# Reordering the products of the whole Strassen pairs in a hybrid decoder step

## Chip, cores and metric

The kernel runs as one program on one core of a Trainium2 chip. The metric is device time in microseconds (us), the median of several runs; lower is better.

## What is computed

Two layers of a decoder trunk run for 512 prompt positions and 8 sample positions, 520 columns in all, with a model width of 2048. In each layer a normalised x is multiplied by `w_in` (2048 by 8192); half of the result goes through a short gated convolution, half through a four-head retention with a carried state; the two halves, joined, are multiplied by `w_out` (2048 by 2048) and added to x; then `x = x + sigmoid(x @ w_pg) * (p @ w_ple)`.

```python
z = h @ w_in
b_c, c_c, x_c, g_c, q, k, v, g_r = split_projection(z)
y_conv = b_c * conv_y * jax.nn.silu(g_c)
y_ret = (o * gn_g.astype(jnp.float32)).astype(x.dtype) * jax.nn.silu(g_r)
x = x + jnp.concatenate([y_conv, y_ret], axis=-1) @ w_out
x = x + jax.nn.sigmoid(x @ w_pg) * (p_i @ w_ple)
```

Everything is float32. The three large products take nearly all of the time.

## The kernel before

**Products.** A float32 operand is held as a high part and a rest, both in the type float32r, and each product of tiles is three matmuls (`mm3`, lines 247 to 249): high by high, high by rest, rest by high. Every such matmul has 128 by 128 weights and 260 moving columns (one half of the 520). Weights arrive from HBM as raw float32 tiles in `raw_ring` (32 tiles, so four loads of eight) and are split by `split_w`: ScalarE copies the high part (line 229), VectorE subtracts it (line 230); the parts wait in `split_ring` (60 tiles).

**Pairs.** Output tiles are made two at a time by `pair`. Each pair has a number of rows s that goes through one level of Strassen-Winograd (the function `strassen`): seven block products in place of eight. The rest of the 16 rows, or all 16 when s is 0 (`plain`), is multiplied in the ordinary way. A pair with s of 16, all its rows, is called whole here. The tables `CONVS`, `OUT_ROWS` and `GATES` make 47 of the pairs whole: 13 in the convolution part of each layer, 5 in the `w_out` part of each layer, 6 and 5 in the `w_pg` part. They stand in six unbroken chains.

**The seven products of a whole pair,** each of 24 matmuls (8 tiles, 3 matmuls a tile), go into three PSUM banks called a, b and d, out of five that the class `Banks` deals in the order in which they were given back:

| product | weights | bank | what follows in the text of the kernel |
|---|---|---|---|
| P1 | w11 | a | ScalarE copies a into d |
| P2 | w21 + w22 - ... | b | ScalarE copies b to the right half of z1 |
| P3 | combination | a, on top of P1 | ScalarE copies a to the right half of z0 |
| P4 | w12 | d, on top of the copy | ScalarE copies d to the left half of z0; one step of other work (`aside`) |
| P5 | w11 - w21 | a, on top | VectorE adds a to the right half of z1 |
| P6 | w12 - combination | b, on top | VectorE adds b to the right half of z0 |
| P7 | w22 | a, on top | ScalarE copies a to the left half of z1 |

Copies and additions out of PSUM are lines of the helpers `copy` and `plus`; both are recorded under line 307. The combinations of raw weights are made in place by VectorE (`add`, line 319). After P7 the three banks go back together, in the order d, b, a. A raw slot goes back when the last product that reads it has been split: w12 after P4, w11 after P5, w21 after P6, w22 after P7.

**What sets the order.** The kernel's text isn't the order of execution. The program is built with `schedule_with_timeline_sim=True`: a planner walks a simulated timeline and gives each engine its own order, by priority. A line that stands earlier in the text has the higher priority; splits of weights and weight sums are lifted by `WPRIO`, and copies and additions out of PSUM go to the front (`high_priority`). Each engine then executes its list in that order. So a product can start ahead of one that stands before it in the text when that one isn't ready in the simulation. Loads of weights are issued by SyncE (line 312 for Strassen pairs, line 222 for ordinary rows).

**Around the pairs.** `middle` and `later` are lists of small jobs (building operands of the next large product, loading and updating the sample group's state, retention steps, the small `w_ple` product) that `strassen` calls at fixed places of its text.

Of the kernel before, what the change touches and what calls it, by code (L numbers as in the profile page):

```python
# [15 lines left out]
KT = D // P  # L16
# [63 lines left out]
class Slots:  # L80
# [8 lines left out]
    def get(self, dtype=F32):  # L89
        i = self.free.pop(0)  # L90
        self.count += 1
        t = self.pool.tile([P, T], dtype, tag=f"s{i}", name=f"slot{i}_{self.count}")
        self.used[id(t)] = (t, i)
        return t
# [97 lines left out]
def trunk_kernel(  # L192
# [17 lines left out]
    get, getr, put = slots.get, slots.getr, slots.put  # L210
    raw_ring = Ring(const, RAW, F32, "raw", 8)
    split_ring = Ring(const, SPLIT, F32R, "split")
    banks = Banks(pg, 5)
# [11 lines left out]
    def split_w(raw, slot=False):  # L225
        n = raw.shape[1]
        hi, lo = (getr()[:, :n] if slot and not split_ring.fits(n // P) else split_ring.get(n // P) for _ in range(2))
        with tc.high_priority(offset=WPRIO):
            S.activation(hi, raw, AF.Copy)  # L229
            V.tensor_tensor(lo, raw, F(hi), SUB)  # L230
        return hi, lo

    def chunks(a, b, most=CH):

        n = (b - a + most - 1) // most
        e = [a + (b - a) * i // n for i in range(n + 1)] if n else [a]
        return list(zip(e, e[1:]))

    def parts(src, a, b, slot=False):
        raw = load(src[:, P * a : P * b])  # L240
        w = split_w(raw, slot)
        raw_ring.put(raw)
        return w
# [7 lines left out]
    LEFT, RIGHT = slice(0, TH), slice(TH, T)  # L251

    def product(out, w, c, xs, start, stop, more=False):

        for i, (xh, xl) in enumerate(xs):
            m = slice(P * (c + i), P * (c + i) + P)
            mm3(out, w[0][:, m], w[1][:, m], xh, xl, start and i == 0, stop and i == len(xs) - 1, more)

    def at(ops, ks, n):
        return [ops[k].view(n) for k in ks]  # L260

    def acc(n):
        return [banks.get() for _ in range(n)]

    def aside():

        if later:
            later.pop(0)()
# [18 lines left out]
        aside()  # L287
        return Val(banks.put, ps=ps[:2]), Val(banks.put, ps=ps[2:])

    def strassen(x, src0, src1, s, step=None):  # L290

        q = s // 2
        ops = x.ops
        x.supply(min(s + CH, KT))
        assert len(x.sums) >= q
        k1, k2 = at(ops, range(0, s, 2), LEFT), range(1, s, 2)
        t1, t2, t3, t4 = ([t[i] for t in x.sums[:q]] for i in range(4))
        step = step or (lambda n: None)  # L300
        a, b, d = acc(3)
        c = banks.get() if s < KT else None
        z0, z1 = get(), get()

        def early(fn, *args):
            with tc.high_priority():
                fn(*args)  # L307

        def raws(src, first):
            w = raw_ring.get(q)  # L310
            for i, j in chunks(0, q, CHL):
                DMA.dma_start(w[:, P * i : P * j], src[:, P * (first + i) : P * (first + j)])
            return w

        def add(out, x, y, op):
            for i, j in chunks(0, q, CHA):
                n = slice(P * i, P * j)
                with tc.high_priority(offset=WPRIO):
                    V.tensor_tensor(out[:, n], x[:, n], y[:, n], op)  # L319

        def times(out, raw, xs, start, more):
            for i, j in chunks(0, q, CHS):
                w = split_w(raw[:, P * i : P * j])
                product(out, w, 0, xs[i:j], start and i == 0, j == q, more)
                split_ring.put(*w)

        def copy(out, ps):
            early(S.activation, out, ps, AF.Copy)

        def plus(out, x, y):  # L330
            early(V.tensor_tensor, out, x, y, ADD)

        w11 = raws(src0, 0)
        times(a, w11, k1, True, False)
        step(1)
        copy(d, a)
        w21, w22 = raws(src1, 0), raws(src1, q)  # L340
        add(w11, w11, w21, SUB)
        add(w21, w21, w22, ADD)
        times(b, w21, t1, True, False)
        step(2)
        copy(z1[:, RIGHT] if c is None else c, b)
        add(w21, w22, w11, SUB)
        times(a, w21, t2, False, True)
        step(3)
        copy(z0[:, RIGHT], a)
        w12 = raws(src0, q)  # L350
        add(w21, w12, w21, SUB)
        times(d, w12, at(ops, k2, LEFT), False, True)
        raw_ring.put(w12)
        step(4)
        if c is None:
            copy(z0[:, LEFT], d)
        aside()
        times(a, w11, t3, False, True)
        raw_ring.put(w11)
        step(5)  # L360
        if c is None:
            plus(z1[:, RIGHT], a, z1[:, RIGHT])
        else:
            copy(z1[:, LEFT], a)
        while middle:
            middle.pop(0)()
        times(b, w21, at(ops, k2, RIGHT), False, True)
        raw_ring.put(w21)
        step(6)
        if c is None:  # L370
            plus(z0[:, RIGHT], b, z0[:, RIGHT])
        times(a, w22, t4, False, True)
        raw_ring.put(w22)
        step(7)
        for i, j in chunks(s, KT):
            last = j == KT
            x.supply(min(j + CH, KT))
            p1, p0 = parts(src1, i, j), parts(src0, i, j)
            product(c, p1, 0, at(ops, range(i, j), RIGHT), False, last, True)
            product(a, p1, 0, at(ops, range(i, j), LEFT), False, last, True)  # L380
            split_ring.put(*p1)
            product(d, p0, 0, at(ops, range(i, j), LEFT), False, last, True)
            product(b, p0, 0, at(ops, range(i, j), RIGHT), False, last, True)
            split_ring.put(*p0)
        if c is not None:
            plus(z1[:, RIGHT], c, z1[:, LEFT])
            copy(z0[:, LEFT], d)
            plus(z0[:, RIGHT], b, z0[:, RIGHT])
            banks.put(c)
        copy(z1[:, LEFT], a)  # L390
        banks.put(d, b, a)
        step(8)
        aside()
        return Val(put, slot=z0), Val(put, slot=z1)

    def pair(x, src, m, n, nxt=None):


        s = x.rows[n]
        last = n == len(x.rows) - 1 and nxt is not None  # L400
        if s:
            z = strassen(x, src[m], src[m + 1], s, (lambda i: x.free(i, nxt)) if last else None)
        else:
            z = plain(x, src[m], src[m + 1], (lambda a, b: x.free_tiles(a, b, nxt)) if last else None)
        x.release(n + 1)
        if nxt is not None and not last and not x.todo:
            nxt.fill(1, PRE)
        return z
# [14 lines left out]
    class Operands:  # L423


        def __init__(self, rows, load, reserve=0, whole=False, gain=None):
            self.rows, self.load, self.reserve, self.whole, self.gain = rows, load, reserve, whole, gain
            self.sent = []
            self.ops = [None] * KT
            self.sums = []  # L430
            self.ready = 0
            first = max(rows[0], min(FIRST, max(rows))) // 2
            self.todo = [(True, True)] * first + [(True, False)] * (KT // 2 - first)
            self.todo = [(i, *t) for i, t in enumerate(self.todo)]
            self.todo += [(i, False, True) for i in range(first, max(rows) // 2)]
# [239 lines left out]
    for a, b in ((0, 1), (1, 4), (4, 8), (8, 12), (12, 16)):  # L675
        raws = []
        if b == 1:
# [3 lines left out]
            x = get()  # L681
# [3 lines left out]
            w = split_w(raw)  # L685
            ws = [[t[:, P * m : P * m + P] for t in w] for m in range(4)]
        else:
            for i in range(4):
                raws.append(load(wi[0, i, :, P * a : P * b]))
                if i < b - a:  # L690
                    x = get()
# [24 lines left out]
    for l in range(DEPTH):  # L716
# [27 lines left out]
        def times(out, z, table):  # L744
            for n, v in z:
                V.tensor_tensor(out[:, n], v, table[:, n], MUL)  # L746
# [54 lines left out]
        def head(m):  # L801
            middle.append(lambda: X.fill(MORE_HEAD, 0))
            if m // 2 % 2:
                middle.append(sample)
            zs = pair(X, wi[l], m, m // 2 - skipped)
            X.fill(MORE_HEAD, 0)
            X.need(m // 2 - skipped + 1)
            sample()
            return zs
# [365 lines left out]
        for m in range(0, KT - tail, 2):  # L1175
# [19 lines left out]
            for i, z in enumerate(zs):  # L1195
                x = xs[i]
# [18 lines left out]
        if tail:  # L1215
            for t in Gt.sums:
                put(*t[4])
            ops = Gt.ops
# [27 lines left out]
            for j, n in enumerate(blocks):  # L1246
                c = slice(PC * j, PC * j + PC)
# [34 lines left out]
            for i in range(tail):  # L1282
                ps = banks.get(TF)
                for c, w in enumerate(ws):
                    for k in range(2):
                        o, m = ops[2 * c + k], slice(PC * k + P * i, PC * k + P * i + P)
                        mm3(ps, w[0][:, m], w[1][:, m], o.x[:, n0], o.y[:, n0], c + k == 0, c + k == 8)
                x = x2[m0 + i][:, n0]
# [38 lines left out]
            for j, n in enumerate(blocks):  # L1327
# [18 lines left out]
                c, q = slice(PC * j, PC * j + PC), slice(j, j + 1)  # L1346
                x = xts[:, c]
# [131 lines left out]
```

## Time and profile before

| | |
|---|---|
| three runs | 2167.43, 2169.55 and 2171.86 us, median 2169.55 |
| the profiled execution | span 2167.3 us, from its first to its last instruction; it has no other time of its own |
| TensorE matmul busy | 2147.8 us, 99% of the span, 17861 instructions |
| TensorE weight load busy | 2142.1 us |
| VectorE busy | 1896.1 us, 87% |
| ScalarE busy | 1264.5 us, 58% |
| GpSimd busy | 430.6 us, 20% |
| bytes moved by DMA | 387.31 MB, mean 179 GB/s |

The busy time of an engine is the union of its instructions' spans; matmul ends are modelled and overlap, so idle time under some 0.15 us between two matmuls doesn't show as idle. In rows of waits, an arrow names what ended the idle time.

### The profile page before, as it was taken

How to read it: one execution, taken by the hardware profiler on the slowest of the kernel's cores; microseconds unless marked ns; L12 is line 12 of the kernel's file. 1: busy time of each engine (PE TensorE's matmuls, PEld its weight loads, DVE VectorE, ACT ScalarE, POOL GpSimd, SP SyncE). 2: the span in 40 equal slices, each digit the busy share in tenths (PEclk: the TensorE clock that was granted, in tenths of full speed). 3: DMA queues.
4: the chain of work that ended last, by engine and by line, in shares of the span. 5: the costliest groups of instructions: out<-in, count | busy, mean ns of one | idle time of the engine just before them, and what ended most of it. 6: DMA issues, size and time to landing. Idle time of an engine off the chain costs nothing. (4 is left out here: it accounts for less than half of the span.)

```text
span 2167.3 us, 48178 instructions
## 1 busy us (share of the span) xinstructions
PE 2147.8 (99%) x17861; PEld 2142.1 (99%) x17861; DVE 1896.1 (87%) x3849; ACT 1264.5 (58%) x2647; POOL 430.6 (20%) x746
## 2 busy tenths in 40 slices
PE   9999999999999999999999999999999999999998
PEld 9999999999999999999999999999999999999998
DVE  8889988998999987987997988989999998879884
ACT  8656655565555655655765655565645555456565
POOL 2313222211001211200212222231111022011011
PEclk9999999999999999999999999999999999999999
DMA  8555565545543745645645566664464355566455
GB/s 288 171 175 197 181 217 184 178 157 175 158 129 118 238 156 187 215 154 160 215 144 175 172 213 191 189 209 170 151 182 149 120 158 202 176 207 200 128 164 198
DMA packets 182861, 387.31 MB, mean 179 GB/s; under 512 B 25888, under 2 KB 56352, under 8 KB 182624
## 3 DMA queue, kind: packets, MB, share of 16 engines
q1 hardware_dynamic: 128704, 212.98, 31.6%
q0 software_dynamic: 53056, 169.84, 23.8%
q8 instruction: 140, 2.29, 0.4%
q10 hardware_dynamic: 864, 1.39, 0.2%
q14 instruction: 97, 0.79, 0.1%
HBM read 318.96 MB, written 65.15 MB: 177 GB/s over the span
## 5 line engine op out<-in xcount | busy, mean ns | idle before, releaser
L247 PE MATMUL ps_g<-slot,split 128*128 128x260 f32 x5465 | 1531.6, 284 | 7.2 <-ACT slot L307 2.9
L248 PE MATMUL ps_g<-slot,split 128*128 128x260 f32 x5465 | 1534.3, 282 | 0.3 <-DVE slot L555 0.3
L249 PE MATMUL ps_g<-slot,split 128*128 128x260 f32 x5461 | 1519.9, 283 | 0.5 <-DVE split L230 0.5
L229 ACT ACTIVATE split<-raw 128x512 fp32r<-128x512 f32 (+2 forms) x1347 | 777.3, 596 | 583.1 <-DVE raw L319 213.2
L247 PEld LDWEIGHTS ps_g<-slot,split 128*128 128x128 f32 x5465 | 1024.0, 188 | 10.1 <-ACT slot L307 3.7
L248 PEld LDWEIGHTS ps_g<-slot,split 128*128 128x128 f32 x5465 | 1028.5, 188 | 0.5 <-DVE slot L555 0.5
L249 PEld LDWEIGHTS ps_g<-slot,split 128*128 128x128 f32 x5461 | 1019.8, 188 | 1.0 <-DVE split L230 1.0
L230 DVE TENSOR_TENSOR split<-raw,split 128x512 fp32r<-128x512 f32 (+2 forms) x1346 | 849.2, 652 | 172.5 <-PE ps_g L248 85.4
L319 DVE TENSOR_TENSOR raw<-raw 128x512 f32<-128x512 f32 (+1 forms) x660 | 428.9, 660 | 32.5 <-DMA raw<-wi 23.7
L307 ACT ACTIVATE slot<-ps_g 128x260 f32<-128x260 f32 x336 | 127.4, 381 | 140.6 <-PE ps_g L249 122.7
L551 ACT ACTIVATE slot<-slot 128x520 fp32r<-128x520 f32 (+1 forms) x212 | 109.2, 562 | 46.6 <-DVE slot L414 11.1
L552 DVE TENSOR_TENSOR slot<-slot,slot 128x520 fp32r<-128x520 f32 (+1 forms) x212 | 124.4, 620 | 4.1 <-ACT slot L551 3.9
L781 POOL DMA_DIRECT2D o_rets<-slot x64 | 35.3, 552 | 351.6 <-DVE slot L780 131.7
L307 DVE TENSOR_TENSOR slot<-ps_g,slot 128x260 f32<-128x260 f32 x168 | 70.9, 424 | 6.0 <-PE ps_g L249 3.7
L869 POOL DMA_DIRECT2D slot<-hs x64 | 46.2, 724 | 118.7 <-DVE split L230 42.7
L814 POOL DMA_DIRECT2D hs<-slot x64 | 35.6, 556 | 139.3 <-DVE slot L755 61.3
L780 DVE SCALAR_TENSOR_TENSOR slot<-slot,vs,slot 128x256 f32<-128x256 f32 x128 | 56.1, 481 | 4.5 <-ACT slot L776 4.3
L746 DVE TENSOR_TENSOR slot<-slot,slot 128x520 f32<-128x520 f32 x80 | 55.8, 698 | 4.7 <-DMA o_rets<-slot 3.7
L770 POOL DMA_DIRECT2D slot<-sret x64 | 35.5, 554 | 114.6 <-ACT split L229 37.3
L1058 POOL DMA_DIRECT2D slot<-x1s x76 | 40.8, 538 | 87.6 <-PE ps_g L249 27.2
L1209 POOL DMA_DIRECT2D x2s<-slot x30 | 16.4, 545 | 201.6 <-DVE slot L1204 200.6
L771 POOL DMA_DIRECT2D slot<-kq x64 | 34.9, 547 | 106.0 <-DVE slot L876 22.2
(217 smaller groups left out, 1733.8 us busy)
## 6 DMA issues: line engine op xcount, KB each, us to landing
raw<-wi SPq DMA_DIRECT2D x377, 256.0 KB, 3.9
raw<-wo SPq DMA_DIRECT2D x128, 256.0 KB, 5.4
raw<-wg SPq DMA_DIRECT2D x122, 256.0 KB, 4.1
raw<-wi SPq DMA_DIRECT2D x136, 192.0 KB, 4.0
slot<-x1s POOLq DMA_DIRECT2D x76, 260.0 KB, 5.1
slot<-sret POOLq DMA_DIRECT2D x64, 256.0 KB, 4.0
hs<-slot POOLq DMA_DIRECT2D x64, 256.0 KB, 4.0
slot<-hs POOLq DMA_DIRECT2D x64, 256.0 KB, 5.2
```

Source lines behind the costliest of these rows:

```text
L229: S.activation(hi, raw, AF.Copy)
L230: V.tensor_tensor(lo, raw, F(hi), SUB)
L247: PE.matmul(out, wh, xh, start=start, stop=False, skip_group_check=more)
L248: PE.matmul(out, wh, xl, start=False, stop=False, skip_group_check=more)
L249: PE.matmul(out, wl, xh, start=False, stop=stop, skip_group_check=more)
L307: fn(*args)
L319: V.tensor_tensor(out[:, n], x[:, n], y[:, n], op)
L551: keep(S.activation(hi, src[:, n], AF.Copy))
L552: V.tensor_tensor(lo, src[:, n], F(hi), SUB)
L746: V.tensor_tensor(out[:, n], v, table[:, n], MUL)
L780: keep(V.scalar_tensor_tensor(st[:, c], k, vs[:, h, e, b : b + 1], st[:, c], MUL, ADD))
L869: SIDE.dma_start(t[:, :512].rearrange("p (m n) -> p m n", m=2), src)
```

## The change

In a whole pair the sixth product P6 is put ahead of the fifth P5 in the text. The first product of the next pair (with its copy from a to d) is made by a function `begin`, and is called inside the present pair between P5 and P7 when the next pair is whole too (`ahead`), at least two banks are free, and the operands are there; the next pair then takes the two banks and the weights from `x.begun`. Bank d goes back right after its copy behind P4, b right after its addition behind P6, and a after P7. For pairs that aren't whole the order of the text stays, and so do all counts of instructions, bytes and sums. Of the 47 whole pairs, 41 are followed by a whole one.

```diff
-    def strassen(x, src0, src1, s, step=None):
+    def strassen(x, src0, src1, s, step=None, ahead=None):
...
+        whole = s == KT
...
-        a, b, d = acc(3)
-        c = banks.get() if s < KT else None
-        z0, z1 = get(), get()
-
...
-        w11 = raws(src0, 0)
-        times(a, w11, k1, True, False)
+        def begin(src):
+            a, d = acc(2)
+            w = raws(src, 0)
+            times(a, w, k1, True, False)
+            copy(d, a)
+            return a, d, w
+
+        a, d, w11 = x.begun or begin(src0)
+        x.begun = None
+        b = banks.get()
+        c = None if whole else banks.get()
+        z0, z1 = get(), get()
         step(1)
-        copy(d, a)
         w21, w22 = raws(src1, 0), raws(src1, q)
...
         if c is None:
             copy(z0[:, LEFT], d)
+            banks.put(d)
         aside()
+        if whole:
+            times(b, w21, at(ops, k2, RIGHT), False, True)
+            raw_ring.put(w21)
+            step(6)
+            plus(z0[:, RIGHT], b, z0[:, RIGHT])
+            banks.put(b)
         times(a, w11, t3, False, True)
         raw_ring.put(w11)
         step(5)
-        if c is None:
+        if whole:
             plus(z1[:, RIGHT], a, z1[:, RIGHT])
         else:
             copy(z1[:, LEFT], a)
         while middle:
             middle.pop(0)()
-        times(b, w21, at(ops, k2, RIGHT), False, True)
-        raw_ring.put(w21)
-        step(6)
-        if c is None:
-            plus(z0[:, RIGHT], b, z0[:, RIGHT])
+        if not whole:
+            times(b, w21, at(ops, k2, RIGHT), False, True)
+            raw_ring.put(w21)
+            step(6)
+        elif ahead is not None and len(banks.free) > 1 and all(ops[0:KT:2]):
+            x.begun = begin(ahead)
         times(a, w22, t4, False, True)
         raw_ring.put(w22)
         step(7)
...
             banks.put(c)
+            banks.put(d, b)
         copy(z1[:, LEFT], a)
-        banks.put(d, b, a)
+        banks.put(a)
...
-            z = strassen(x, src[m], src[m + 1], s, (lambda i: x.free(i, nxt)) if last else None)
+            z = strassen(x, src[m], src[m + 1], s, (lambda i: x.free(i, nxt)) if last else None,
+                         src[m + 2] if s == KT and x.rows[n + 1 : n + 2] == [KT] else None)
```

## Rows read from the trace of the kernel before

**Rows 1.** The page: busy time by engine; busy tenths and granted clock in 40 slices.

```profile
PE 2147.8 (99%) x17861; PEld 2142.1 (99%) x17861; DVE 1896.1 (87%) x3849; ACT 1264.5 (58%) x2647; POOL 430.6 (20%) x746
...
PEclk9999999999999999999999999999999999999999
```

**Rows 2.** Windows: six stretches with the 47 whole pairs; busy us (instructions), clock, DMA.

```profile
444.00:696.00 252.00, 251.06 (x2099) 250.88 (x2098) 230.61 (x458) 139.56 (x281) 32.93 (x47) 1.00 0.48 147
...
919.00:1057.00 138.00, 138.00 (x1154) 138.00 (x1154) 112.56 (x207) 78.80 (x151) 14.44 (x27) 1.00 0.51 159
1513.00:1766.00 253.00, 252.57 (x2105) 251.74 (x2104) 232.88 (x463) 139.06 (x282) 32.80 (x47) 1.00 0.48 146
...
sum 960.00, PE 958.46 PEld 957.25 DVE 832.99 ACT 526.33 POOL 119.31; mean PE 159.74 PEld 159.54 DVE 138.83 ACT 87.72 POOL 19.88
```

**Rows 3.** Waits of TensorE, whole span: us in total, times, longest.

```profile
PE ps_g L247 <- ACT slot L307: 2.9, 4, 1.3
PE ps_g L247 <- ACT ps_g L307: 1.6, 2, 1.2
...
PE ps_vt L913 <- DMA slot<-hs: 0.9, 1, 0.9
...
PE ps_g L247 <- DVE slot L307: 0.2, 1, 0.2
```

**Rows 4.** Waits of TensorE in the stretch from 1513 to 1766 us.

```profile
PE ps_g L247 <- ACT split L229: 0.2, 1, 0.2
```

**Rows 5.** Timeline of TensorE in a pair of `w_out`: start us, duration us.

```profile
868.40 0.28 PE L249 MATMUL ps_g<-slot,split 128*128 128x260 f32 x1
868.52 0.28 PE L247 MATMUL ps_g<-slot,split 128*128 128x260 f32 x1
```

**Rows 6.** Timeline of ScalarE, last whole pair of the first `w_out`: copies out of PSUM.

```profile
858.76 0.39 ACT L307 ACTIVATE slot<-ps_g 128x260 f32<-128x260 f32 x1 [0.80 <-PE ps_g L249]
...
861.64 0.39 ACT L307 ACTIVATE slot<-ps_g 128x260 f32<-128x260 f32 x1 [0.80 <-PE ps_g L249]
```

**Rows 7.** Timeline of VectorE, the same pair: the addition behind P5.

```profile
865.08 0.42 DVE L307 TENSOR_TENSOR slot<-ps_g,slot 128x260 f32<-128x260 f32 x1
```

**Rows 8.** Timeline of ScalarE, a whole pair of the first convolution and its neighbours' joins.

```profile
561.16 0.37 ACT L307 ACTIVATE slot<-ps_g 128x260 f32<-128x260 f32 x1
...
561.95 0.38 ACT L307 ACTIVATE ps_g<-ps_g 128x260 f32<-128x260 f32 x1
...
580.92 0.39 ACT L307 ACTIVATE slot<-ps_g 128x260 f32<-128x260 f32 x1 [0.58 <-PE ps_g L249]
...
581.73 0.38 ACT L307 ACTIVATE ps_g<-ps_g 128x260 f32<-128x260 f32 x1
```

**Rows 9.** The loads of line 312 from issue to landing: stretches 444 to 696, 770 to 870.

```profile
DMA to landing us min/median/max: 2.6/3.5/6.8
...
DMA to landing us min/median/max: 3.0/5.6/7.2
```

**Rows 10.** Waits of VectorE and ScalarE for TensorE: 820 to 900, then 560 to 660.

```profile
DVE split L230 <- PE ps_g L248: 8.4, 12, 0.8
...
ACT split L229 <- PE ps_g L249: 14.2, 12, 2.2
```

**Rows 11.** Waits of TensorE from 700 to 731 and from 1785 to 1797 us.

```profile
PE ps_g L247 <- ACT split L229: 1.3, 1, 1.3
PE ps_g L247 <- ACT ps_g L307: 1.2, 1, 1.2
PE ps_g L247 <- ACT slot L307: 0.8, 1, 0.8
...
PE ps_g L247 <- ACT slot L307: 1.9, 2, 1.3
```

**Rows 12.** Timeline of ScalarE ahead of the wait that ends at 706.46 us.

```profile
702.89 2.31 ACT L551 ACTIVATE slot<-slot 128x260 fp32r<-128x260 f32 x5
...
706.03 0.37 ACT L307 ACTIVATE ps_g<-ps_g 128x260 f32<-128x260 f32 x1
```

More of the change, by code (lines that the diff above doesn't have):

```diff
@@ L430, in __init__ @@
             self.sums = []
+            self.begun = None
             self.ready = 0
```

## The prediction

> **What bounds the kernel now.** I read the page first. TensorE is busy for 99% of the span with matmuls and as long with weight loads, VectorE for 87%, and the granted clock stands at the top of its scale in all 40 slices [rows 1]. So the question for any reordering is how much of TensorE's time is waiting, and where.
>
> The second view cuts the span into stretches. The change touches whole pairs alone, and the 47 of them lie in six stretches that I cut at their chains' ends: 960.00 us together, in which matmuls are busy for 958.46 us [rows 2]. The reader is to see the difference, 1.54 us: that is all the visible idle time of TensorE in every place that the change edits. In the stretches of `w_out` and in the first of `w_pg` there is none at all.
>
> The third view, the waits, names what is in those 1.54 us. The longest, 0.9 us, is a retention step that waits for a load of old keys and values (ps_vt); it has nothing to do with the pairs. What is left is 0.2 us for a split of weights [rows 4] and 0.2 us for VectorE's addition out of PSUM [rows 3]. The larger waits on copies out of PSUM in the list of the whole span, 2.9 and 1.6 us [rows 3], fall mainly elsewhere: 5.2 us of waits stand where the convolution's last pair ends and the first, ordinary pair of `w_out` begins, once in each layer [rows 11].
>
> A busy engine can still be slow inside, so the fourth view is the pitch from matmul to matmul: 868.40 to 868.52, 0.12 us [rows 5]. Two copies that stand behind two consecutive products of 24 matmuls start 858.76 and 861.64 us, 2.88 us apart, again 0.120 us a matmul [rows 6]: the join between two products in two banks costs nothing over the pitch. Seven products are 168 matmuls, 20.2 us a pair, and no order of products makes that less.
>
> **The change, part by part.**
>
> *Counts.* Matmuls, splits, weight sums, copies and bytes stay as they are: 0.
>
> *P6 ahead of P5, next P1 ahead of P7.* The planner already does much of this. In a convolution pair, the copy behind the old pair's P7 (561.16) and the copy of the new pair's a into d, which follows its P1 (561.95), start 0.79 us apart; at the other end of the pair they do so again, 580.92 and 581.73 [rows 8]. Were P1 executed after P7, they would stand at least 2.88 us apart. So the two products are already interleaved, and the new text mostly writes down an order that is being executed. What can be won is the wait of P7 for the addition behind P5: 0.2 us in the whole span [rows 3], taken as won: -0.2 us.
>
> *Banks given back early.* A new product waits for its bank only where the copies in the lists of waits stand; inside the six stretches no wait on line 307's copies by ScalarE is listed and the additions are the 0.2 us already counted. Worth 0. The Trainium skill (Perfetto Trace Analysis, section Matmuls) advises rotating independent groups through different banks so that evacuation overlaps the next group. By that rule more rotation should help; the trace says that three banks of five already hide every copy, so by the trace the sum gets nothing from it.
>
> *The ends of the chains.* This is where the change can cost. Six whole pairs have no whole successor, so there the text goes P6, P5, P7 with no P1 between, and P7 accumulates in bank a, which VectorE must first have read behind P5. Before, P6 covered that with 2.88 us. In the last whole pair of `w_out` P4's copy starts at 861.64 and P5 is the next product, so its result is ready for a reader at about 861.64 + 2.88 = 864.52; the addition runs from 865.08 for 0.42 us, to 865.50 [rows 6, 7]. Uncovered, that is 865.50 - 864.52 = 0.98 us of idle TensorE at each end, with P7 and everything behind it in TensorE's list held up; the longest wait of any kind on line 307 is 1.3 us [rows 3]. Six ends give between 0 (the planner fills the gap with the next pair's P1, an ordinary product, as it fills gaps today) and 6 x 1.3 = 7.8 us. I take 0.2 us each, the one wait on this addition that the trace shows, since the filler that the planner uses now is still there: +1.2 us.
>
> *The fourth load of a pair.* Four loads of eight tiles fill the raw ring, so w12 of the next pair goes into the slot of this pair's w22, which is free once P7's weights are split. In the old text three products (P1, P2, P3 of the next pair, 8.6 us) lie between that and P4; in the new one two (5.8 us), for P1 has gone ahead. A load of line 312 lands after a median of 3.5 us in the convolution and 5.6 in `w_out`, at most 6.8 and 7.2 [rows 9]. So most loads still fit, and some come up to 7.2 - 5.8 = 1.4 us late for the sum and the splits behind them. TensorE needn't see that: in `w_out` VectorE's splits wait for TensorE to give split slots back (8.4 us in 80), and in the convolution ScalarE's do (14.2 us in 100) [rows 10], so the splits run ahead of TensorE by as much as their ring holds. From 0 to 41 x 1.4 = 57 us; I take 0, for the ahead-running splits.
>
> *The queues.* The new P1 gets priority over P7 and over the arithmetic behind the pair. The loads of w11 move ahead with it on SyncE's queue, past none of the loads of the same pair. GpSimd's loads keep their place. VectorE has 960 - 833 = 127 us free in the stretches, ScalarE 434 [rows 2], and they get no more work: 0.
>
> Sum: 2167.3 - 0.2 + 1.2 = 2168.3 us for the span. The median of the runs was 2169.55, 2.25 us over the profiled span of 2167.3, so the time is 2170.5 us. Within 0.2%, 4.3 us, is about what a measurement of this kernel can't tell from no change; the three runs themselves spread over 4.4 us.
>
> **The rivals.**
>
> *Slower: uncovered additions at the ends of the chains.* The place is between P5 and P7 of six pairs, the price 0.98 to 1.3 us each. For it: TensorE takes matmuls in its list's order, and the planner's simulated delay need not be the chip's 0.98 us. The Trainium skill (PSUM - Partial Sum Buffer, section Engine vs sequencer instructions) says that matmuls start in program order, and the rows of waits agree: an idle TensorE ends with the one thing it waited for. Against it: the next pair's product is independent. With nothing filled, 6 x 1.3 = 7.8 us and 2177.4 us; it decides above 4.3 / 6 = 0.72 us an end.
>
> *Slower: w12 comes late.* Half a microsecond at each of the 24 convolution pairs with a whole successor would give 12 us, 2181.6 us; 0.18 us each already decides. Against it stand the medians of landing and the waits for split slots.
>
> *Slower: a new order brings a copy behind other work elsewhere.* The wait that ends at 706.46 shows the mechanism: ScalarE spent 2.31 us on five operand splits from 702.89, and the copy into bank d began only at 706.03 [rows 12]. Four such waits of 1.2 us more, 2174.4 us.
>
> *Faster: the 5.2 us behind the convolutions go.* The planner re-plans the whole program, and a change of priorities earlier may put those copies ahead of the operand splits. All of it gone would be 2169.55 - 5.2 = 2164.4 us. Against it: none of the lines edited stands there, since the pairs at that place are not whole.
>
> *Nothing happens.* If the planner arrives at nearly its old lists, 2169.5 us; this is on the same side as the forecast.
>
> **How the numbers follow.** No change within 0.2%: 0.62. Uncovered ends: 0.13. Late w12: 0.08. Copies behind other work: 0.05. Waits behind the convolutions gone: 0.12. So faster 0.12, same 0.62, slower 0.26. The range goes from 2163.5, just below the faster case, to 2178, over the first slower case; it leaves out late loads and the outer part of the others, some 0.15. The likeliest case's own range is 2166 to 2174.
>
> **What would show it.** Right: the six stretches keep TensorE idle for under 4 us in all, pairs follow each other every 20.2 us, the next pair's copy of a into d starts some 2.9 us ahead of the copy behind P7, and the granted clock stays at the top. Each step could be seen wrong: waits on the addition of line 307 at six places (ends of chains), waits of line 319 and line 229 on raw loads that pass on to TensorE (late w12), or a drop of the waits between the convolution and `w_out`. The prediction would be wrong if TensorE's time hid slack that no row here shows as idle, or if the re-planned lists differ far from the places edited.

## The result and the profile after

The changed kernel takes 2188.41 us (2185.0 to 2190.08, 4 runs) against 2169.03 us before, a ratio of 1.0088 with a 95% interval of 1.0073 to 1.0102: 19.4 us slower, outside the predicted range and on the side that had 0.26.

The page of the changed kernel (line 304 stands for the old 307, 316 for 319, 309 for 312). First its busy times, then the group of the weight sums (busy us, mean ns, idle us before them and what ended it):

```profile
PE 2155.3 (99%) x17861; PEld 2145.3 (98%) x17861; DVE 1895.9 (87%) x3849; ACT 1267.5 (58%) x2647; POOL 440.3 (20%) x746
...
L316 DVE TENSOR_TENSOR raw<-raw 128x512 f32<-128x512 f32 (+1 forms) x660 | 425.5, 655 | 76.5 <-DMA raw<-wg 42.7
```

The instruction counts are those of [rows 1], and VectorE works no longer than before. New is that VectorE stood idle for 42.7 us ahead of weight sums because weights of `w_pg` (wg) hadn't landed.

Windows of the changed kernel, columns as in [rows 2]: the first `w_pg` chain, then the first `w_out` chain.

```profile
924.00:1072.00 148.00, 144.31 (x1185) 142.29 (x1184) 115.87 (x219) 78.50 (x155) 15.79 (x30) 1.00 0.50 152
...
774.00:878.00 104.00, 104.00 (x869) 104.00 (x868) 79.41 (x135) 52.37 (x101) 13.45 (x25) 1.00 0.56 177
```

The same edit leaves no idle time in the `w_out` chain (104.00 of 104.00 us busy) and costs in `w_pg` (148.00 - 144.31 = 3.69 us idle, where [rows 2] has none). Waits of TensorE in the changed kernel, longest first:

```profile
PE ps_g L247 <- DVE slot L304: 5.0, 10, 1.8
PE ps_g L247 <- ACT slot L568: 4.5, 3, 2.6
PE ps_g L249 <- DVE split L230: 4.0, 8, 0.7
PE ps_g L247 <- ACT ps_g L304: 2.5, 2, 2.3
```

The wait of P7 for VectorE's addition went from 0.2 us [rows 3] to 5.0 us in ten places, and third matmuls of a tile (line 249, which read the rest of a weight) wait for VectorE's splits.

Visible idle time misses short delays, so I also summed, over all matmuls, how much later than 121 ns each started after the one before it, by the section of the program that it belongs to. This is worked out from the matmul starts in the trace (us; the names of the experiments are below):

```text
section            before  changed  own_ring  wp_first  others_old  old_own  late_start
layer 1 heads       10.93    10.78     11.29     10.63       10.35    10.82       10.93
layer 1 convolution  6.01     7.28      5.92      5.54        5.41     4.97        3.31
layer 1 w_out        3.58     6.65      7.00      6.72        5.33     4.96        7.20
layer 1 w_pg         1.41     7.85      1.48      1.44        5.37     1.15        1.15
layer 2 heads        5.80     9.23     10.04      8.20        8.18     5.98        7.27
layer 2 convolution  6.86     4.87      4.96      7.04        7.20     6.92        3.60
layer 2 w_out        1.76     3.77      3.77      7.49        3.43     3.43        3.43
layer 2 w_pg         4.16     8.14      4.28      5.27        7.48     3.58        3.75
sum                 40.52    58.57     48.75     52.32       52.74    41.81       40.65
```

Of the 18.05 us more, 10.4 stand in the two `w_pg` sections, 5.1 in the `w_out` sections (whose first pair is an ordinary one) and 3.4 in the heads of layer 2, where no pair is whole. Changes of some 2 us in a section are small: two controls below show them at an unchanged total.

**The clock.** Two stretches of the changed kernel ran at a granted clock of 0.50 (1.2 GHz in place of 2.4):

```profile
449.20:452.40 3.20, 3.20 (x17) 3.20 (x16) 3.20 (x9) 1.02 (x4) 0.25 (x1) 0.50 0.30 91
739.30:742.50 3.20, 3.20 (x16) 3.20 (x16) 3.20 (x7) 2.57 (x5) 0.77 (x3) 0.50 0.59 146
```

TensorE counts as busy there, but starts 16 or 17 matmuls where 26 fit at 121 ns. Shortly before each stretch it had stood idle, 1.78 us for an addition (to 447.60) and 2.6 us for an operand split (to 737.85); a wait of 2.3 us at 1235 was not followed by a fall. The matmul starts put 2.9 of the 18.05 us in the two stretches, one in the first convolution and one in the first `w_out`. In the kernel before the clock stood at 1.00 in all the stretches of [rows 2].

**What happens in a w_pg pair.** Timeline of VectorE around the join of two pairs of the first `w_pg`, changed kernel:

```profile
1012.86 1.28 DVE L230 TENSOR_TENSOR split<-raw,split 128x512 fp32r<-128x512 f32 x2
1016.88 0.69 DVE L316 TENSOR_TENSOR raw<-raw 128x512 f32<-128x512 f32 x1 [2.75 <-DMA raw<-wg]
1017.49 0.69 DVE L230 TENSOR_TENSOR split<-raw,split 128x512 fp32r<-128x512 f32 x1
1018.10 0.42 DVE L304 TENSOR_TENSOR slot<-ps_g,slot 128x260 f32<-128x260 f32 x1
...
1019.03 0.69 DVE L230 TENSOR_TENSOR split<-raw,split 128x512 fp32r<-128x512 f32 x1
...
1020.30 0.42 DVE L304 TENSOR_TENSOR slot<-ps_g,slot 128x260 f32<-128x260 f32 x1
```

and of TensorE:

```profile
1019.77 0.39 PE L249 MATMUL ps_g<-slot,split 128*128 128x260 f32 x1 [0.64 <-DVE split L230]
1020.78 0.39 PE L247 MATMUL ps_g<-slot,split 128*128 128x260 f32 x1 [0.27 <-DVE slot L304]
```

VectorE stands for 2.75 us ahead of a sum whose weights aren't there. Behind it in VectorE's order stand a split and the two additions out of PSUM, which come at 1018.10 and 1020.30. The split that ends at 1019.72 releases the first wait of TensorE, the addition that ends at 1020.72 the second. The Trainium skill (PSUM — Partial Sum Buffer, section Engine vs sequencer instructions) calls VectorE's queue strictly first in, first out; the trace agrees, for additions whose bank was long complete didn't overtake the sum.

Why the weights are late is seen in the loads. The listing joins the trace's landing times with the program's order, for the first tiles of each load of the next pair, in the same place of both kernels (us):

```text
before                 slot freed by               freed   issued   landed  first read
w11'                   split for P5               994.96   994.99   998.69     1002.50
w21'                   split for P6               996.79   996.81  1001.34     1004.61
w22'                   split for P7               999.66   999.68  1003.74     1006.28
changed
w11'                   split for P4              1000.97  1001.04  1004.30     1006.50
w21'                   split for P5              1005.93  1005.96  1010.02     1010.12
w22'                   split for P7              1013.54  1013.57  1016.86     1016.88
```

In `w_pg` the small `w_ple` product loads four raw tiles through the same ring, half a slot. With four slots, w22' then gets the slot of the present pair's w22 in both kernels, and waits for P7's split. Before, P7's split was followed by P1's; now P1's split is already done, and w22' is read at once, for the sum ahead of P2. Before, it lay ready for 2.5 us; now it is read 0.02 us after it landed.

One view of the whole chain shows the reversal. VectorE's longest wait in the first `w_pg` chain, the changed kernel:

```profile
DVE raw L316 <- DMA raw<-wg: 22.9, 11, 3.0
```

and the kernel before, from 919 to 1057 us:

```profile
DVE split L230 <- PE ps_g L248: 22.7, 25, 1.9
```

VectorE used to be ahead and wait for TensorE to give back split slots; now it is behind and waits for loads from HBM.

### The profile page after: what moved, and what is told of

Same layout as the page of the kernel before. It is cut to its first block, busy times and chain, and to the rows that moved or that the text cites. A ratio compares the mean times of both kernels' runs of the same rounds, so it can differ in the third digit from the quotient of the medians.

```text
span 2186.8 us, 48337 instructions
## 1 busy us (share of the span) xinstructions
PE 2155.3 (99%) x17861; PEld 2145.3 (98%) x17861; DVE 1895.9 (87%) x3849; ACT 1267.5 (58%) x2647; POOL 440.3 (20%) x746
## 5 line engine op out<-in xcount | busy, mean ns | idle before, releaser
L316 DVE TENSOR_TENSOR raw<-raw 128x512 f32<-128x512 f32 (+1 forms) x660 | 425.5, 655 | 76.5 <-DMA raw<-wg 42.7
L304 ACT ACTIVATE ps_g<-ps_g 128x260 f32<-128x260 f32 x121 | 44.9, 371 | 22.1 <-PE ps_g L249 21.8
```

## The experiments

Every ratio is against runs of the kernel before on the same chip. The experiments stood on several chips, on which the kernel before had medians of 2167.65 to 2169.03 us, so a difference of two totals can be off by 1.4 us for that alone. Letters name the theories in the quoted expectations.

### No early begin in w_pg: no_begin_wpg

```diff
...
-            zs = pair(Gt, wg[l], m, m // 2, X)
+            zs = pair(Gt, wg[l], m, m // 2, X, early=False)   # ahead is None
```

> The changed kernel, but in the w_pg part no next pair is begun early; P6 still stands ahead of P5 and the banks still go back early. Theory A (the early begin takes a raw slot, so that loads of the next pair land late in the w_pg chains, VectorE sits in its order on a weight sum, and the additions out of PSUM behind it come late): some 10 us of the changed kernel's 19 us go, 2178 us, and VectorE's idle time on loads of wg falls from 42.7 us to under 10. Rival B (P6 ahead of P5 is the cause, it halves the cover of w12's sum): 2188 us, the waits in w_pg stay.

Measured: 2179.77 us, 1.0054 (1.0039 to 1.0069), 8.6 us less than the changed kernel. VectorE waits 3.3 us for wg in place of 42.7. Theory A holds; P6-first alone doesn't make the waits of `w_pg`.

### No early begin at all: no_begin

```diff
-                         src[m + 2] if s == KT and x.rows[n + 1 : n + 2] == [KT] else None)
+                         None)
```

> The changed kernel without any early begin: P6 ahead of P5 and the banks given back early alone. Theory A: as without the begin in w_pg, and what else the begins cost goes too, 2172 to 2178 us. Rival B: 2185 us or more. Rival C (the loss is spread by re-planning, whichever part is edited): anything from 2170 to 2190, with waits at new places that no edit touches.

Measured: 2175.8 us, 1.0032 (1.0020 to 1.0043), inside A's band and inside C's wide one too. Here P7 follows P5 in the text of all 47 pairs, and still its list of waits holds no addition out of PSUM by VectorE; the longest are these:

```profile
PE ps_g L247 <- ACT slot L568: 6.5, 3, 3.1
PE ps_g L247 <- ACT slot L304: 2.7, 2, 2.1
```

The planner fills the gap behind P5, so the rival of the prediction that I priced at the chains' ends isn't what costs here. The longest wait is for operand splits by ScalarE (line 568), and it stands in the ordinary first pair of each `w_out` part, which no edit touches: there C is right. Behind one wait of each line the clock was halved again.

### Raw tiles of its own for w_ple: own_ring

```diff
+    ple_ring = Ring(const, 4, F32, "ple")
...
-            later.append(lambda m=m, w=parts(wp[l, m // 2], 0, 4), pes=pes: embed(m, w, pes))
+            raw = ple_ring.get(4)
+            DMA.dma_start(raw, wp[l, m // 2])
+            w = split_w(raw)
+            ple_ring.put(raw)
+            later.append(lambda m=m, w=w, pes=pes: embed(m, w, pes))
```

> The changed kernel, with the raw tiles of the small w_ple product in four tiles of their own instead of the shared raw ring. Theory A1 (the ring of four slots is one too few only because the w_ple load takes half a slot just when the begun pair holds one more): the w_pg loss goes, 2178 us. Rival A2 (the early begin alone makes the loads late, whoever shares the ring): 2188 us, VectorE still waits over 30 us for wg.

Measured: 2177.81 us, 1.0038 (1.0023 to 1.0053): 10.6 us less than the changed kernel, with every early begin still in place. The two `w_pg` sections fall from 15.99 to 5.76 us of delay. VectorE's wait:

```profile
DVE raw L317 <- DMA raw<-wg: 2.8, 4, 1.0
```

The early begin is harmless in `w_pg` once w22' can take another slot.

### The w_ple load ahead of the begin: wp_first

```diff
+            while soon:
+                soon.pop(0)()              # next pair's w_ple load
             x.begun = begin(ahead)
...
```

> The changed kernel, with the w_ple load of the next pair written just ahead of the early begin instead of behind it; the ring stays as it is, shared and of 32 tiles. The half slot then goes out first, and no weight of the sum ahead of P2 gets the slot of the pair's own w22. Theory A2 (what is late is the load that is dealt w22's slot): the w_pg loss goes as with tiles of its own, 2178 us, VectorE's idle time on wg under 10 us. Rival A1 (the ring is half a slot too small, in any order): 2185 us or more, over 30 us of idle.

Measured: 2180.76 us, 1.0065 (1.0050 to 1.0080). The total lies 7.7 us below the changed kernel, 5 by the two ratios; 8.0 us of idle VectorE on wg in all; no wait of TensorE is left in the first `w_pg` chain, and the delay of both sections is 6.71 us for 15.99. The ring is as small as before, so A2 holds: what counts is which load is dealt w22's slot. The total missed the expected 2178, since the second `w_out` section grew from 3.77 to 7.49 us, at a place that this edit doesn't touch.

### The kernel before with the w_ple load behind P1: wp_late

```diff
         times(a, w11, k1, True, False)
+        while soon:
+            soon.pop(0)()                  # this pair's w_ple load
         step(1)
...
```

> The kernel before, with the w_ple load written behind the pair's first product, so that the slots are dealt as in the changed kernel, but no pair is begun early: the third load of a pair waits for the split of P7 with one product of cover, where the changed kernel leaves none. Theory A2: VectorE waits some 10 to 25 us for wg, and TensorE loses 0 to 4 us, 2169 to 2173. Rival (dealing alone makes the loss): 2179 us. Rival (dealing is harmless without the begin): under 3 us of idle on wg.

Measured: 2166.67 us, 1.0000 (0.9991 to 1.0010), and 1.9 us of VectorE waiting for wg. The first expectation fell, and the last rival's 1.9 us is what came. The premise was off too: w22' already had w22's slot in the kernel before, as the loads above show, and with P1 between P7's split and the read that was enough. The loss needs the shared ring and the begin together.

### The begin without P6-first: old_p5first

```diff
             times(a, w11, t3, False, True)      # P5
...
+            times(b, w21, at(ops, k2, RIGHT), False, True)   # P6, as before
+            x.begun = begin(ahead)
...
```

> Of the change the begin without P6-first: P5, P6, begin, P7 in whole pairs, the w_ple tiles in the shared ring, pairs that are not whole in the old text. Theory A: the w_pg loss stays as in the changed kernel, some 10 us, so 2179 to 2184 us with over 30 us of VectorE waiting for wg. Rival B: P6-first was needed for the loss, so 2172 us.

Measured: 2175.47 us, 1.0035 (1.0022 to 1.0048). VectorE waits 47.0 us for wg, and the `w_pg` sections have 15.32 us of delay, as A says. The median is below A's band; the profiled run, 2179.50 us, is in it. The order of P5 and P6 isn't the cause in `w_pg`. It does cost in this plan, elsewhere: others_old, the next kernel, differs from this one in that order alone (and so in where `middle` stands), and is 8.3 us slower, with intervals that don't meet, though its `w_pg` sections have less delay (12.85 us).

### Old text for pairs that are not whole: others_old

```diff
+        else:
+            a, b, d = acc(3)
+            c = banks.get()
+            z0, z1 = get(), get()
+            w11 = raws(src0, 0)
+            times(a, w11, k1, True, False)
+            step(1)
+            copy(d, a)
...
```

> The changed kernel, but pairs that are not whole get their banks and their first copy in the old order of the text; the plan is then the old one up to the first whole pair. Theory C (re-planning of the heads and of the pairs around w_out costs some 7 us of the 19): 2182 us. Rival (all of the loss comes from whole pairs): 2188 us.

Measured: 2183.79 us, 1.0069 (1.0054 to 1.0084), 4.6 us less. The single runs hardly overlap (2181.30 to 2185.26 against 2185.00 to 2190.08), the two intervals do. The change had also moved the text of the pairs with 8, 12 or 14 rows: the copy from a to d ahead of `step(1)`, and b and c taken behind P1. The longest wait in the heads of layer 2, 2.3 us of TensorE for a copy into d, is gone with the old text. By section, though, only 1.1 of the 5.8 us that go stand in those heads, and 3.1 in `w_pg`, whose whole pairs the edit doesn't touch.

### That text alone in the kernel before: others_new

The reverse of the edit above, with nothing else of the change.

> The kernel before, with the new text for the pairs that are not whole alone: banks a and d first, the copy right behind P1, b and c after it. Theory C1 (this text itself costs, most of it in the heads of the second layer): 2173 to 2175 us. Rival C2 (what it cost in the changed kernel was the luck of one plan): 2167 to 2171 us.

Measured: 2169.67 us, 1.0010 (1.0001 to 1.0020). By itself it costs 2 us, in C2's band. So the 4.6 us in the changed kernel are no fixed price: most of them belong to that plan.

### Two controls: ctl_banks and ctl_deal

```diff
-        banks.put(d, b, a)
+        banks.put(b, d, a)      # ctl_banks
...
-        a, b, d = acc(3)
+        a, d, b = acc(3)        # ctl_deal
```

> A control: the kernel before, with b and d given back in the other order at the end of a pair (b, d, a). Nothing that waits is changed, only the numbers of the banks that the next pair gets. Theory C (any re-plan moves the time by some us): 2165 to 2175 us, clear of 2169 by more than 2 us, with waits at other places. Rival (re-planning is neutral): 2169 us within 1.

> A second control: the kernel before with a, d, b dealt in this order in every pair, nothing else moved. If the numbers of the banks matter by themselves, the part of C1 that is dealing shows here, 2173 us; if not, 2169 us within 2, with waits at other places than before.

Measured: 2168.56 us, 0.9999 (0.9990 to 1.0009), and 2168.86 us, 1.0012 (1.0002 to 1.0021). The totals hold within 1.2 us, so "any re-plan moves the time by some us" fell. The sections don't hold still: the heads of layer 2 have 8.00 and 7.71 us of delay for 5.80, the convolution of layer 2 4.74 and 5.46 for 6.86.

### Both repairs: old_own

`own_ring` and `others_old` in one kernel.

> Both repairs together: the pairs that are not whole in the old text, and four raw tiles of its own for the w_ple product; begin and P6-first stay. If the two costs are separate they add: 2188 - 10.6 - 4.6 = 2173 us. If what is left of the loss is made by the begins or by P6-first themselves: 2176 us or more.

Measured: 2171.89 us, 1.0014 (1.0004 to 1.0023). The two costs add within the noise: 10.6 us for the ring, 5.9 more for the text of the other pairs (2177.81 - 2171.89), and 3.0 are left (2171.89 - 2168.93). Waits of TensorE:

```profile
PE ps_g L248 <- ACT slot L577: 4.6, 3, 1.9
PE ps_g L248 <- DVE slot L305: 3.3, 2, 1.9
```

The 3.3 us on additions are P7 of the first whole pair in each convolution chain, 1.46 and 1.85 us; behind the second the clock was halved once (1.4 us of delay). The changed kernel has the same waits, there 1.78 and 0.97 us. VectorE and then TensorE, first convolution, changed kernel:

```profile
440.16 1.29 DVE L316 TENSOR_TENSOR raw<-raw 128x512 f32<-128x512 f32 x2 [2.39 <-DMA raw<-wi]
...
447.12 0.42 DVE L304 TENSOR_TENSOR slot<-ps_g,slot 128x260 f32<-128x260 f32 x1
```

```profile
447.60 0.39 PE L247 MATMUL ps_g<-slot,split 128*128 128x260 f32 x1 [1.78 <-DVE slot L304]
```

It looks like the mechanism of `w_pg` once more: a sum for the pair begun early, weights not there, the addition behind it late. The next two runs test it.

### No begin in the first convolution pair, and none in the convolution: late_start and no_conv

```diff
-                         src[m + 2] if s == KT and x.rows[n + 1 : n + 2] == [KT] else None)
+                         src[m + 2] if s == KT and x.rows[n + 1 : n + 2] == [KT] and (x is not X or x.rows[n - 1] == KT) else None)   # late_start
+                         src[m + 2] if s == KT and x.rows[n + 1 : n + 2] == [KT] and x is not X else None)   # no_conv
```

> Both repairs (w_ple tiles of their own, old text for pairs that are not whole), and in the convolution the first whole pair of the chain begins no successor; all later ones do. Theory D (what is left of the loss is the addition behind P5 in that first pair, late because VectorE sits on a weight sum whose load has not landed: 1.5 and 1.9 us with both repairs): these two waits go, 2169 us, no different from the kernel before. Rival (the wait moves to the next pair that begins one): 2172 us and a wait on the addition some 20 us later.

> Both repairs, and no early begin in the convolution at all; in w_out and w_pg it stays. Theory D: no wait on the additions out of PSUM over 0.3 us anywhere, 2169 us. Rival (the rest of the loss is re-planning around the first pair of w_out): 2171 to 2174 us, with the waits there, as without any begin.

Both stand on old_own. Measured: 2169.68 us, 1.0005 (0.9996 to 1.0014), and 2169.66 us, 1.0010 (1.0001 to 1.0019). The waits on additions are gone in both, and both are within 0.1% of the kernel before: D holds for the waits. The totals by themselves don't part these runs from old_own, for the intervals overlap.

In late_start the convolutions have 6.91 us of delay for 12.87 before, yet the time isn't below that of before. The first `w_out` section has 7.20 for 3.58. Timeline of ScalarE, then TensorE, at its first pair:

```profile
734.25 0.73 ACT L577 ACTIVATE slot<-slot 128x260 fp32r<-128x260 f32 x2 [5.18 <-DMA slot<-ys]
```

```profile
734.72 0.39 PE L248 MATMUL ps_g<-slot,split 128*128 128x260 f32 x1 [3.48 <-ACT slot L577]
```

TensorE waits there for an operand that the retention left in HBM (ys), and runs at half the clock behind it (1.5 of the 7.20 us).

### P6-first alone: old_nobegin

Both the old text for the other pairs and `ahead` always None; the ring is shared.

> Of the whole change only P6 ahead of P5 and the early return of b and d in whole pairs; no begin, and the pairs that are not whole in the old text. Theory A (begin with the shared ring, and re-planning): 2169 to 2172 us, and waits at the six chain ends and the 41 other pairs on the addition behind P5 of under 3 us in all. Rival B (P6-first uncovers that addition before P7, now in all 47 pairs): 0.5 us a pair, over 2180 us.

Measured: 2176.14 us, 1.0036 (1.0024 to 1.0049), above A's band, though no wait on an addition is in its list and the convolutions are down to 7.23 us of delay. What it loses stands at the first pairs of `w_out`: 13.73 us of delay in the two sections for 5.34, the longest wait for an operand split of ScalarE 3.1 us. Of the 13.73, 3.0 us are matmuls at half the clock, behind two of these waits. B's mechanism is dead, though P6-first and the early return of banks alone cost 7.2 us. Why this plan loses there more than no_conv, which has P6-first in every pair too, stays open.

Summed in the same way, the two `w_out` sections have 8.4 to 15.9 us of delay in all ten kernels with P6 ahead of P5, and 5.0 to 7.6 in the six without. The new order also puts the jobs of `middle` behind both products, where they stood between them; no run moved one without the other, so whether either of them makes the operand splits late isn't shown.

## Why the prediction was wrong

**The fourth load.** This is the step that failed. I counted four loads in a ring of four slots, found that w12 gets w22's slot, and took 0 because the splits run ahead. A late load was the right mechanism, but it came in another load and in a part that I hadn't looked at: in `w_pg` the `w_ple` load makes five users, so the load behind P7's split is w22', which the sum ahead of P2 reads with no product of cover. The slack of 2.5 us it had before was the P1 that the change moved away. A ring of its own for `w_ple` gave back 10.6 us of the 19.4; I had taken 0. My cover by "splits run ahead" [rows 10] was read in `w_out` and the convolution; it held in the `w_out` chains and is itself what the late load uses up.

**The pairs that aren't whole.** I said that none of the edited lines stands in them, and the section on the change says that their text stays. The diff moved their first copy and two banks all the same. In the changed kernel this was worth 4.6 us (5.9 once the ring was repaired), by itself 2 us; I had 0.

**P6 ahead of P5.** I took -0.2 us. Alone, with the early return of banks, it costs 7.2 us (old_nobegin), and 8.3 with the begin and the shared ring (others_old against old_p5first); with both repairs no more than 3.0 us are left in all, so this price belongs to the plan too, and its cause is open.

**P7's addition.** I priced it at the six ends of the chains, +1.2 us. In the changed kernel it is 0.46 us there, at one end (P7 at 1068.74 us, the first `w_pg`). It is longer at the starts of the two convolution chains (1.78 and 0.97 us), where a pair begun early brings sums forward whose weights haven't landed. With both repairs 3.0 us of loss are left, and without those two waits 1.8 (late_start and no_conv), a step within the noise.

**The clock.** I expected it at the top throughout. It was halved in two stretches behind long waits, 2.9 us of delay in all, which my prices for waits left out.

**Right:** all counts stayed, and the pitch of TensorE at the full clock; no order of the products came out faster than the kernel before; `w_out` chains kept pairs without idle time; no wait on a bank showed anything of their early return, which wasn't run by itself.

**Open:** why plans differ by 8 us in the `w_out` sections (13.73 in old_nobegin, 5.34 before). The half clock is 3.0 us of it, the order of P5 and P6 or the place of `middle` goes with the rest, and only one wait was followed to a load (ys).

## What to carry to other kernels

Moving work of an engine forward moves its loads' deadlines too: for each buffer ring, list every user in the changed order, small ones included, and for each load name the read that frees its slot and the work between that and its own first read. An engine with a tenth of its time free can still hold up a saturated one when an instruction that isn't ready stands ahead in its order, so where VectorE changes from waiting for TensorE to waiting for DMA, look there first for TensorE's loss (it need not come: 5.2 us of such waits cost TensorE nothing in the first `w_pg` chain of wp_first). Where idle time in the edited places is 1.5 us of 2167, an edit can win next to nothing there, and its risk lies in what it moves.

## What the runs showed that was not expected

TensorE's loss was a quarter of VectorE's wait: 42.7 us of idle VectorE on wg came out as 10.4 us of delay in `w_pg`; that what VectorE's splits had laid in covered the rest is likely, but wasn't followed split by split. And two re-deals of the PSUM banks moved delays of up to 2.2 us between sections while the total stayed within 1.2 us.
